# Modulation pieces moved to other stages, a five-bank rotation for the output projection and gate, and a held transpose in a two-block transformer kernel

## The chip, the cores and the metric

The kernel runs on one core of a Trainium2 chip as a single launch. The metric is device time in microseconds (us), the median of several executions. A separate profiled execution gives the trace. TensorE is written PE (its weight loads PEld), VectorE DVE, ScalarE ACT, GpSimd POOL and SyncE SP; SP issues every DMA of this kernel.

## The reference, cut to what matters

The input x is 1024 tokens by 1024 features, all float32. Two blocks follow each other.

```python
def reference(...):
    x = first_block(...)    # one layer
    return second_block(...)  # two layers
# first_block
proj = rms_norm(x, g) @ w_in
ya = diff_attention(...)            # 4 heads, dense
yb = neighbourhood_attention(...)   # 8 heads
x = x + concat(ya, yb) @ w_out
x = x + sigmoid(x @ w_ple_gate) * (p @ w_ple_proj)
# second_block, for l in 0, 1
mod = silu(c) @ w_mod[l] + b_mod[l]          # 1024 -> 6 * 1024
sh1, sc1, gt1, sh2, sc2, gt2 = split(mod, 6)
h = rms_norm(x, g1) * (1 + sc1) + sh1
o = concat(dilated_attention(h), latent_attention(h))
x = x + gt1 * (o @ w_out[l])
h = rms_norm(x, g2) * (1 + sc2) + sh2
x = x + gt2 * (relu(h @ w_mlp_in[l]) ** 2 @ w_mlp_out[l])
```

`mod` has one row, so it is not worth a matrix product on PE: the kernel computes it on DVE.

## The kernel before, in words

Every float32 product runs as three PE products of a high and a low part (`mm3`); ACT makes the high part and DVE or POOL the low part (`split`, `load_w`). One accumulation over 1024 features is 24 matmuls of 512 columns into one PSUM bank. The eight banks are pools of their own: two G (`psum_g`), two S (`psum_s`), one A (`psum_a`), two T and one J (`psum_t`).

The stages in order: attention of the first block; its output projection (`block1_end` calls `out_proj`) and its gate (`halves` with its own `mul`); then for each layer l the dilated heads (`dilated`), the latent heads (`mla`, four pairs hp of two heads), the output projection (`out_proj`), the up projection (`mlp`: two plain products per half, then groups fg 1 to 15) and the down projection (`down_proj`: 35 steps of four 9-matmul runs, then a plain tail).

**Modulation pieces.** `mod_start` fills a list, `background`. For each layer it holds 96 pieces and four sums. A piece (`mod_piece`, L967) loads 256 KB of w_mod into a tile `modraw` and multiplies it by silu(c) with one DVE instruction that also accumulates. A sum (`mod_sum`, L973 and L975) ends a range of pieces with two small matmuls and one or two DVE instructions. The main program takes entries off the list with `run_background(n)`: 36 in the first block, 51 in the latent heads of layer 0 (2 for each of the eight half-heads of hp 0 and 1, 4 for those of hp 2, then 4, 4, 5, 6), 42 in its up groups (3 after each of fg 2 to 15), 10 in its down projection (steps 0 to 9), 51 in the latent heads of layer 1, and the last 10 in its up groups, one after each. The tile a piece uses is `self.mraw`: a ring of two in the latent heads, and the ring of two `raw` tiles from the up groups on.

**The planner.** `TileContext(..., schedule_with_timeline_sim=True)` orders each engine's instructions at build time. The place in the program is an instruction's priority (`high_priority(n)`, used by `ahead`, raises it), and an instruction may be put ahead of others where its tiles and operands are free. On the chip each engine, and SP's queue of DMAs, runs its list in order.

**Output projection and gate.** `out_proj` has 16 groups (8 feature tiles by 2 halves of the tokens). Each loads a tile xo, accumulates 24 matmuls in a G bank and ends with one DVE instruction (L875 in the first block, L877 later) that adds xo. In the first block the same DVE also builds the position tables of the dilated heads: 32 instructions at L1156, each followed by a 256 KB DMA out of a ring of two tiles `tab`. The 16 groups of the gate read the sums of the output projection.

**End of the dilated heads.** The last pair's `dil_merge` weighs the outputs on DVE (L1432), adds them on POOL (L1433, tile `mix`) and returns `put`, eight transposes into two G banks, which `pipeline` runs at its end. `mla_start`, which prepares the first latent pair, comes just ahead of that in the program.

Of the kernel before, what the change touches and what calls it, by code (L numbers as in the profile page):

```python
# [11 lines left out]
F32 = mybir.dt.float32  # L12
# [6 lines left out]
P = 128  # L19
# [114 lines left out]
class Emit:  # L134
# [58 lines left out]
    def psum_s(self, shape=None):  # L193
        return self.psS.tile(shape or [P, 512], F32, tag="S", name="sps")

    def psum_a(self):
        return self.psA.tile([P, 512], F32, tag="A", name="pa")

# [72 lines left out]
    def setup(self):  # L271
        nc = self.nc
        es = self.es
        self.dram = self.pool("dram", es, space=DRAM)
        self.const = self.pool("const", es)
        self.psS = self.pool("psS", es, {"S": 2}, PSUM)
        self.psA = self.pool("psA", es, {"A": 1}, PSUM)
        self.psT = self.pool("psT", es, {"T": 2}, PSUM)
        self.psJ = self.pool("psJ", es, {"J": 1}, PSUM)
        self.scaler = nc.gpsimd  # L280
        self.turn, self.apart = 0, False
        self.psG = self.pool("psG", es, {"G": 2}, PSUM)
        self.hp = self.pool("hp", es)
        self.wp = self.pool("wp", es, {"wh": WB, "wl": WB, "raw": 2})
        self.wring = [self.wp]
        self.st = self.pool("st", es, {"l1": 3, "l2": 3, "r24": 2, "rsy": 2, "rst": 2, "sr": 2, "stw": 2, "stc": 2, **{t: 4 for t in ("mn", "cc", "ssq", "r8")}})
        c = self.const
        self.ident = c.tile([P, P], F32, name="ident")
        make_identity(nc, self.ident)
        self.inv24 = c.tile([P, 24], F32, name="inv24")  # L290
        nc.vector.memset(self.inv24[:, 0:16], 1.0 / 64)
        nc.vector.memset(self.inv24[:, 16:24], 1.0 / 32)
        self.zeros = c.tile([P, 1], F32, name="zeros")
        nc.vector.memset(self.zeros, 0.0)
        self.mixd = [self.dram.tile([8, P, S], F32, name=f"mixd{b}") for b in range(3)]
        self.xTd = [self.A["x_o"]] + [self.dram.tile([8, P, S], F32, name=f"xTd{b}") for b in (1, 2)]
        self.xTm = self.dram.tile([8, P, S], F32, name="xTm")
        self.modd = {}
# [408 lines left out]
        with self.tc.high_priority(n):  # L707
            return f()

    def pipeline(self, groups, lag=1, ahead=(0, 0, 0, 0)):  # L710


        values, finish, put = [], [], None
        for before, scores, val, fin, after in groups:
            for f in before:
                f()
            if put:
                self.ahead(put, ahead[0])
            put = self.ahead(finish.pop(0), ahead[1]) if len(finish) > len(values) else None
            self.ahead(scores, ahead[2])  # L720
            values.append(val)
            finish.append(fin)
            if len(values) > lag:
                self.ahead(values.pop(0), ahead[3])
            for f in after:
                f()
        while values:
            self.ahead(values.pop(0), ahead[3])
            if put:
                self.ahead(put, ahead[0])  # L730
            put = self.ahead(finish.pop(0), ahead[1])
        for f in finish:
            if put:
                self.ahead(put, ahead[0])
            put = self.ahead(f, ahead[1])
        if put:
            self.ahead(put, ahead[0])

# [126 lines left out]
    def out_proj(self, w, b, gate, order, after, step=lambda: None, done=lambda d, half: None, pair=True):  # L865
        nc = self.nc

        def mul(d, half, wt, c0):
            sl = slice(half * 512, half * 512 + 512)
            xo = self.xt.tile([P, 512], F32, tag="xo", name="xo")  # L870
            self.dma(xo, self.xTd[b][d, :, sl])
            ps = self.psum_g()
            self.gemm_t(ps, self.mix, half, wt, 8, c0, order)
            if gate is None:
                nc.vector.tensor_tensor(self.X(d, half), ps, xo, op=OP.add)  # L875
            else:
                nc.vector.scalar_tensor_tensor(self.X(d, half), ps, gate[:, d:d + 1], xo, op0=OP.mult, op1=OP.add)  # L877
                self.dma(self.xTm[d, :, sl], self.X(d, half))
            done(d, half)

        self.halves(w, mul, after, step, self.first_w, pair)
# [9 lines left out]
    def block1_end(self, after):  # L891
        nc = self.nc
        x1 = self.act()

        def split_x(d, half):
            hi, lo = self.act_tile(x1, d, half)
            self.split(hi, lo, self.X(d, half))

        es = ExitStack()
        self.wring = [self.wp] * WB + [self.pool("gw", es, {"wh": 2, "wl": 2})] * 2  # L900
        pp = self.pool("ple", es, {"gth": 3, "pl": 3})
        tables = self.position_tables(es)
        per = -(-len(tables) // 16)

        def side():
            for _ in range(min(per, len(tables))):
                tables.pop(0)()
            if side_steps.pop(0):
                self.run_background(1)

        side_steps = [True] * 4 + [False] * 99
        self.out_proj(self.A["w_out"][0], 0, None, None, lambda half: None, side, split_x, False)

        def mul(d, half, wt, c0):
            sl = slice(half * 512, half * 512 + 512)
            pl = pp.tile([P, 512], F32, tag="pl", name="ple")
            self.dma(pl, self.pled[d, :, sl])
            ps = self.psum_g()
            self.gemm_t(ps, x1, half, wt, 8, c0)
            th = pp.tile([P, 512], F32, tag="gth", name="gth")  # L920
            nc.scalar.activation(th, ps, AF.Tanh, scale=0.5)
            nc.vector.scalar_tensor_tensor(th, th, 1.0, pl, op0=OP.add, op1=OP.mult)
            nc.vector.tensor_tensor(self.X(d, half), self.X(d, half), th, op=OP.add)
            self.dma(self.xTd[1][d, :, sl], self.X(d, half))

        self.halves(self.A["w_ple_gate"][0], mul, after, side)
        self.wring = [self.wp]
        es.close()
# [3 lines left out]
    def mod_start(self):  # L932
# [12 lines left out]
        for l in range(2):  # L945
            m = c.tile([P, 48], F32, name=f"mod{l}")
            self.dma(m, A["bmod"][l])
            self.mod.append(m)
        for l in range(2):
            done = None  # L950
            for t0, t1 in ((0, 16), (16, 24), (24, 40), (40, 48)):
                for t in range(t0, t1):
                    for h in range(2):
                        self.background.append(lambda l=l, t=t, h=h: self.mod_piece(l, t, h))
                        if done and (t, h) == (t0, 1):
                            self.background.append(done)
                done = lambda l=l, t0=t0, t1=t1: self.mod_sum(l, t0, t1)
            self.background.append(done)
# [302 lines left out]

        return [lambda h=h: rope(h) for h in range(2)] + [lambda k=k, h=h: down(k, h) for k in (2, 0, 1) for h in range(2)]

    def dil_v(self, a, l, g):
        s = {}

        def load():
            s["w"] = self.load_w(self.A["w_in_2"][l], [(1024 + g * 256, 256)], 8)

        def step(tt):  # L1270
            ps = self.psum_g([P, 2, 256])
# [126 lines left out]
    def dil_merge(self, l, pr, stw, stc, o):  # L1398
# [25 lines left out]
        nc.vector.tensor_tensor(F, F, a1.unsqueeze(3).to_broadcast([P, 2, 8, 2]), op=OP.mult)  # L1424
        mixes = []
        for half in range(2):
            mix = self.up.tile([P, 4, P], F32, tag="w2k", name="mix")
            hs = slice(4 * half, 4 * half + 4)
            for m in range(2):
                for x in range(2):  # L1430
# [11 lines left out]
    def dilated(self, a, l):  # L1442
# [44 lines left out]
                    yield before if n == 0 else [], *g, after[n]  # L1487

        self.apart = True
        self.pipeline(groups(), 1, (0, 100, 0, 100))  # L1490
        self.apart = False
        es.close()

# [86 lines left out]
    def mla(self, l):  # L1580
# [6 lines left out]
        def groups():  # L1587
            s = self.mla0[0]
            for hp in range(4):
                cur = s  # L1590
# [7 lines left out]
                for m in range(2):  # L1598
                    T, pre = self.mla_heads(2 * hp + m, cur, m)
                    for half in range(2):  # L1600
                        n = 2 if hp < 2 else 4 if hp < 3 or not m else 5 + half
                        yield [pre] if half == 0 else [], *self.mla_group(l, hp, m, half, T, cur), after[2 * m + half] + [lambda n=n: self.run_background(n)]

        self.pipeline(groups(), 1, (0, 60, 0, 60))
        es.close()
# [111 lines left out]
    def mlp(self, l, close, after):  # L1717
# [112 lines left out]
        with ExitStack() as eu:  # L1830
            up = self.pool("uu", eu, {"r": 8})
            up_rest(1, w, *begun[1], up)
            for fg in range(2, 16):
# [4 lines left out]
                else:  # L1838
                    w = wide(A["w_mlp_in_2"][l], 0, 4, fg * 256, 256)
                up_rest(fg, w, *(begun[fg] if fg in begun else up_first(fg, w, up)), up)  # L1840
                self.run_background(1 if l else 3)
        es.close()
        self.es_sr.close()
        self.down_proj(l, us, u0, add_to, after)
# [2 lines left out]
    def down_proj(self, l, us, u0, add_to, after):  # L1847
# [74 lines left out]
        for n, (c, i) in enumerate(seq):  # L1922
# [2 lines left out]
            if n < 3:  # L1925
                load_x(((0, 1, 4, 5), (2, 3, 6, 7))[n > 0], int(n < 2))
            if l == 0:
                self.run_background(int(n < 10))
            for q in range(2):
                for j in range(2):  # L1930
                    if i == 0:
# [39 lines left out]
    def emit(self, stop=None):  # L1971
        with self.es:
# [9 lines left out]
            for l in range(2):  # L1982
# [6 lines left out]
                ex = ExitStack()  # L1989
                self.open_xt(ex)  # L1990
                self.wring = [self.wp] * WB + [Slots(self.hx, [f"b{j}" for j in range(16, 24)])] * 8
                self.out_proj(self.A["w_out_2"][l], 1 + l, self.mod[l][:, 16:24], (0, 1, 2, 6, 3, 4, 5, 7), lambda half: (self.norm_mlp(half, l), half or self.mlp_first(l)))
                self.mlp(l, ex.close, lambda half: l == 0 and self.norm(half, 1, 0, acts[1]))
            es.close()

# [22 lines left out]
```

## Time and profile before

| | us |
|---|---|
| median of 3 runs (lowest, highest) | 3768.87 (3767.29, 3771.7) |
| profiled execution, its own time | 3776.56 |
| profiled execution, span of the trace | 3774.8 |
| PE busy in the span | 3538.3 |
| DVE busy | 2776.9 |
| ACT busy | 1835.6 |
| POOL busy | 1446.2 |

The profiled execution is 7.7 us longer than the median; its span leaves out 1.76 us of its own time. Times inside the span are given in us from its start. In a window of the trace, an engine's idle time is the window's length less its busy time. The granted clock of PE is a share of 2.4 GHz; at the lower of the two levels, 1.2 GHz, it is 0.5.

### The profile page before, as it was taken

The page shows a single profiled execution, that of the slowest core. Times are in us where ns is not written, and L with a number is a line of the kernel's source. Part 1 is how long each engine was busy: PE and PEld are TensorE (multiplying, and loading weights), DVE is VectorE, ACT ScalarE, POOL GpSimd, SP SyncE. Part 2 cuts the span into 40 slices and gives each one's busy share as a digit, 9 for nine tenths or more (in the row PEclk, how much of TensorE's full clock was granted, in tenths as well). Part 3 has the DMA queues.
Part 4 walks back from the last instruction along what each step waited for, and adds up shares of the span by engine and source line. Part 5 has one row for each costly group of instructions (what it writes and reads, how often), then busy time and mean ns, then how long its engine had stood idle before and what let it go on. Part 6 is the DMA issues. An engine that isn't in the chain of part 4 may idle for free. (4 is left out here: it accounts for less than half of the span.)

```text
span 3774.8 us, 59060 instructions
## 1 busy us (share of the span) xinstructions
PE 3538.3 (94%) x20256; PEld 3044.6 (81%) x20256; DVE 2776.9 (74%) x6238; ACT 1835.6 (49%) x3691; POOL 1446.2 (38%) x1155
## 2 busy tenths in 40 slices
PE   7999899989999899998999999899889998999999
PEld 7899899767998778776787887898767876887887
DVE  7888776564666798739867987666798738667986
ACT  5565555533454667624233443455567734333442
POOL 2111232323322223238666553322232236766552
PEclk8999999999999999999999999899999998999999
DMA  7221222463456540134648542455541143448541
GB/s 234 82 54 51 69 72 74 144 196 120 137 171 172 161 123 26 61 116 141 224 154 284 156 147 80 125 160 164 168 129 45 37 131 107 158 152 282 158 146 64
DMA packets 380988, 497.82 MB, mean 132 GB/s; under 512 B 37392, under 2 KB 216592, under 8 KB 380688
## 3 DMA queue, kind: packets, MB, share of 16 engines
q1 hardware_dynamic: 380688, 494.05, 41.9%
q8 instruction: 160, 2.62, 0.3%
q14 instruction: 140, 1.15, 0.1%
HBM read 336.11 MB, written 115.87 MB: 120 GB/s over the span
## 5 line engine op out<-in xcount | busy, mean ns | idle before, releaser
L247 POOL TENSOR_TENSOR wl<-raw,wh 128x512 fp32r<-128x512 f32 (+2 forms) x226 | 291.8, 1302 | 636.7 <-ACT wh L246 540.4
L174 DVE TENSOR_TENSOR pl<-pt,ph 128x512 fp32r<-128x512 f32 (+3 forms) x409 | 269.9, 665 | 66.5 <-ACT ph L173 54.8
L173 ACT CAST ph<-pt 128x512 fp32r<-128x512 f32 (+3 forms) x409 | 227.4, 571 | 143.6 <-PE pt L691 69.0
L246 ACT CAST wh<-raw 128x512 fp32r<-128x512 f32 (+2 forms) x226 | 133.1, 608 | 226.8 <-DMA raw<-in_w_out_dram 56.2
L967 DVE SCALAR_TENSOR_TENSOR modraw<-modraw,csil 128x512 f32<-128x512 f32 x192 | 174.0, 911 | 32.1 <-DMA modraw<-in_wmod_dram 31.4
L1869 ACT CAST wh<-rq 128x768 fp32r<-128x768 f32 x120 | 99.6, 835 | 151.3 <-PE pg L1940 75.2
L1641 ACT ACTIVATE xm<-xm,mn 128x1024 f32<-128x1024 f32 x128 | 148.2, 1158 | 43.4 <-DVE mn L496 43.1
L404 POOL TENSOR_TENSOR qn<-qn,r 128x512 f32<-128x512 f32 x56 | 61.2, 1097 | 267.5 <-DVE r L168 159.6
L496 DVE CUSTOM_DVE_ANT_0 xd<-sps,dtab 128x256 f32<-128x256 f32 (+1 forms) x256 | 101.4, 411 | 79.1 <-PE sps L1329 60.6
L1870 DVE TENSOR_TENSOR wl<-rq,wh 128x768 fp32r<-128x768 f32 x120 | 156.5, 1308 | 0.4 <-ACT wh L1869 0.4
L1696 DVE TENSOR_TENSOR wl<-ssum,wh 128x1024 fp32r<-128x1024 f32 x60 | 120.4, 2007 | 10.7 <-ACT wh L1695 8.1
L698 PE MATMUL pa<-pl,vpm 128*128 128x512 f32 x256 | 111.4, 435 | 8.5 <-DVE pl L174 7.9
L1695 ACT CAST wh<-ssum 128x1024 fp32r<-128x1024 f32 x60 | 62.8, 1047 | 116.3 <-PE pg L1707 43.4
L1695 ACT CAST wh<-sraw 128x512 fp32r<-128x512 f32 (+1 forms) x58 | 48.1, 830 | 137.8 <-PE pg L1707 67.7
L697 PE MATMUL pa<-ph,vpm 128*128 128x512 f32 x256 | 108.5, 424 | 0.6 <-ACT ph L173 0.4
L691 PE MATMUL pt<-ident,xm 128*128 128x128 f32 x692 | 106.9, 273 | 1.4 <-DVE pl L174 0.5
L1736 DVE SCALAR_TENSOR_TENSOR r<-r 128x512 f32<-128x512 f32 x90 | 104.2, 1158 | 2.3
L462 PE MATMUL sps<-ks,qs 128*128 128x512 f32 (+1 forms) x224 | 90.7, 405 | 14.7 <-DVE mn L496 13.4
L691 PEld LDWEIGHTS pt<-ident,xm 128*128 128x128 f32 x692 | 85.7, 140 | 22.1 <-DVE pl L174 1.1
L496 DVE CUSTOM_DVE_ANT_0 xm<-sps,zeros,mn 128x512 f32<-128x512 f32 x128 | 95.1, 743 | 11.3 <-PE sps L223 10.5
L174 DVE TENSOR_TENSOR pl<-pj,ph 128x512 fp32r<-128x512 f32 (+3 forms) x135 | 88.1, 653 | 19.5 <-ACT ph L173 16.8
L538 ACT ACTIVATE x<-x,mn 128x1024 f32<-128x1024 f32 x64 | 73.8, 1153 | 56.2 <-DVE mn L496 53.0
(1675 smaller groups left out, 13966.1 us busy)
## 6 DMA issues: line engine op xcount, KB each, us to landing
modraw<-in_wmod_dram SPq DMA_DIRECT2D x192, 256.0 KB
sraw<-in_w_mlp_in_dram SPq DMA_DIRECT2D x60, 512.0 KB
us<-r SPq DMA_DIRECT2D x120, 256.0 KB
rq<-in_w_mlp_out_dram SPq DMA_DIRECT2D x80, 384.0 KB
raw<-in_w_in_dram SPq DMA_DIRECT2D x194, 128.0 KB
us<-rc SPq DMA_DIRECT2D x90, 256.0 KB
ks<-khh SPq DMA_DIRECT2D x128, 128.0 KB
dtab<-awd SPq DMA_DIRECT2D x32, 512.0 KB
```

What stands on the lines that cost most here:

```text
L173: nc.scalar.copy(hi, src)
L174: nc.vector.tensor_tensor(lo, src, hi.bitcast(F32), op=OP.subtract)
L246: nc.scalar.copy(wh[:, sl], raw)
L247: nc.gpsimd.tensor_tensor(wl[:, sl], raw, wh[:, sl].bitcast(F32), op=OP.subtract)
L496: self.nc.vector.tensor_tensor_reduce(out=dst, in0=src, in1=bias, scale=1.0, scalar=init, op0=OP.add, op1=OP.min, accum_out=mn)
L691: nc.tensor.transpose(ps[:, (i - base) * P:(i - base + 1) * P], X[i][:, c * P:c * P + P], self.ident)
L698: nc.tensor.matmul(ops[:, sl], v(j), pl[:, sl], start=False, stop=last, skip_group_check=True)
L967: nc.vector.scalar_tensor_tensor(raw, raw, 1.0, self.csil, op0=OP.mult, op1=OP.mult, accum_out=self.macc[:, h, t:t + 1])
L1641: nc.scalar.activation(x, x, AF.Exp, scale=-1.0, bias=mn[:, 1:2], accum_out=T["l"][:, i:i + 1])
L1695: nc.scalar.copy(wh[:, 0:m], x)
L1696: (nc.vector if i < 3 else nc.gpsimd).tensor_tensor(wl[:, 0:m], x, wh[:, 0:m].bitcast(F32), op=OP.subtract)
L1870: eng.tensor_tensor(lo, x, hi.bitcast(F32), op=OP.subtract)
```

## The change

Five things change. `psum_w` hands out five banks in turn (S, G, S, A, G), and `out_proj` and the gate use it in place of `psum_g`. The counts of `run_background` change, and the output projections of the second block take pieces too, in a ring of two tiles `u1`. The last `put` of the dilated heads is not run by their `pipeline` but kept in `self.held` and placed behind the first head's `pre` in `mla`, and its `mix` tiles come from the latent pool's ring `x` of four. Two of a layer's sums come two entries later in the list. `dil_v` gets a parameter that no call uses.

```diff
+    def psum_w(self):
+        self.wide_turn = (self.wide_turn + 1) % 5
+        return (self.psum_g, self.psum_s, self.psum_g, self.psum_s, self.psum_a)[self.wide_turn]()
...
-    def pipeline(self, groups, lag=1, ahead=(0, 0, 0, 0)):
+    def pipeline(self, groups, lag=1, ahead=(0, 0, 0, 0), hold=False):
...
+        if hold:
+            return put
         if put:
             self.ahead(put, ahead[0])
...
# out_proj and the gate in block1_end
-            ps = self.psum_g()
+            ps = self.psum_w()
...
# mod_start
-                        if done and (t, h) == (t0, 1):
+                        if done and (t, h) == (t0 + (t0 > 16), 1):
...
# dil_merge
-            mix = self.up.tile([P, 4, P], F32, tag="w2k", name="mix")
+            mix = self.me.tile([P, 4, P], F32, tag="x", name="mix") if pr == 3 else self.up.tile([P, 4, P], F32, tag="w2k", name="mix")
...
# dilated
-        self.pipeline(groups(), 1, (0, 100, 0, 100))
+        self.held = self.pipeline(groups(), 1, (0, 100, 0, 100), True)
...
# mla
-                        n = 2 if hp < 2 else 4 if hp < 3 or not m else 5 + half
-                        yield [pre] if half == 0 else [], *self.mla_group(l, hp, m, half, T, cur), after[2 * m + half] + [lambda n=n: self.run_background(n)]
+                        n = ((0, 0, 3, 4) if l else (0, 1, 4, 5 + m))[hp]
+                        before = [] if half else [pre] if hp or m else [pre, self.held]
+                        yield before, *self.mla_group(l, hp, m, half, T, cur), after[2 * m + half] + [lambda n=n: self.run_background(n)]
...
# mlp, after each fg from 2
-                self.run_background(1 if l else 3)
+                self.run_background((fg > 5) * (1 if l else 4))
...
# down_proj, layer 0, step n
-                self.run_background(int(n < 10))
+                self.run_background(int(2 < n < 34))
...
# emit, each layer
+                self.mraw = (self.mq, "u1")
+                left = [5, 5]
+                def side():
+                    if left:
+                        self.run_background(left.pop())
-                self.out_proj(..., lambda half: (self.norm_mlp(half, l), half or self.mlp_first(l)))
+                self.out_proj(..., lambda half: (self.norm_mlp(half, l), half or self.mlp_first(l)), side)
```

`side` is called after every two groups of the output projection.

## Rows read from the trace of the kernel before

**Rows 1.** The page, part 1: busy time, share of the span and instructions.

```profile
PE 3538.3 (94%) x20256; PEld 3044.6 (81%) x20256; DVE 2776.9 (74%) x6238; ACT 1835.6 (49%) x3691; POOL 1446.2 (38%) x1155
```

**Rows 2.** Windows: length, busy (instructions) by engine, granted clock, DMA share, GB/s.

```profile
755.57:828.13 72.56, 59.40 (x241) 46.60 (x239) 43.01 (x69) 17.13 (x33) 20.24 (x14) 0.95 0.68 220
...
1287.00:1312.00 25.00, 18.20 (x120) 16.38 (x119) 24.15 (x66) 14.53 (x41) 16.68 (x20) 0.80 0.24 77
2722.00:2745.00 23.00, 14.80 (x99) 12.95 (x99) 22.31 (x64) 12.15 (x34) 16.71 (x19) 0.78 0.26 83
1590.00:1677.00 87.00, 85.16 (x391) 69.81 (x390) 30.65 (x49) 24.61 (x41) 29.95 (x24) 1.00 0.39 125
```

**Rows 3.** Windows of the latent heads, up groups and down projection, same columns.

```profile
1300.00:1412.00 112.00, 103.37 (x584) 81.98 (x583) 110.76 (x304) 76.21 (x158) 41.25 (x46) 0.95 0.42 128
...
1737.00:1875.00 138.00, 121.93 (x493) 97.38 (x494) 120.61 (x156) 42.48 (x59) 101.81 (x60) 0.93 0.69 227
1875.00:2025.00 150.00, 150.00 (x663) 124.25 (x662) 93.73 (x73) 47.44 (x68) 98.21 (x70) 1.00 0.49 172
2075.00:2350.00 275.00, 275.00 (x1217) 227.84 (x1216) 225.80 (x267) 108.53 (x165) 131.79 (x73) 1.00 0.40 125
2740.00:2850.00 110.00, 97.79 (x567) 75.81 (x565) 107.53 (x297) 73.83 (x154) 38.20 (x41) 1.00 0.41 122
...
3165.00:3210.00 45.00, 40.35 (x164) 32.09 (x163) 40.86 (x39) 14.37 (x21) 38.93 (x23) 0.92 0.57 187
```

**Rows 4.** Windows of the tile modraw alone: length, DVE busy (two instructions a piece).

```profile
1300.00:1412.00 112.00, 37.72 (x98) 0.95 0.42 128
1737.00:1875.00 138.00, 58.09 (x100) 0.93 0.69 227
2740.00:2853.00 113.00, 37.69 (x98) 1.00 0.40 119
3165.00:3210.00 45.00, 13.52 (x18) 0.92 0.57 187
```

**Rows 5.** Line L967, the piece on DVE: duration ns min/median/max.

```profile
L967 DVE SCALAR_TENSOR_TENSOR modraw<-modraw,csil x192: 656/690/1782, 35.0 to 3201.9; 128x512 f32<-128x512 f32 x192
```

**Rows 6.** Waits from 725 to 940 us: engine line, for whom, total, times, longest.

```profile
DVE tab L1156 <- DMA acd<-tab: 23.5, 18, 3.0
PEld pg L221 <- DVE xT L875: 15.6, 7, 4.1
PE pg L221 <- DVE xT L875: 15.2, 7, 3.7
```

**Rows 7.** PE timeline: first matmuls of output projection groups (start, us, idle before).

```profile
755.57 0.39 PE L221 MATMUL pg<-a01h,wh 128*128 128x512 f32 x1
...
782.64 0.80 PE L221 MATMUL pg<-a01h,wh 128*128 128x512 f32 x1 [3.71 <-DVE xT L875]
...
828.13 0.50 PE L221 MATMUL pg<-a00h,wh 128*128 128x512 f32 x1 [1.32 <-DVE xT L875]
...
844.60 0.39 PE L221 MATMUL pg<-a00h,wh 128*128 128x512 f32 x1
```

**Rows 8.** PE timeline at the end of the dilated heads, layer 0 and layer 1.

```profile
1297.00 1.12 PE L201 MATMUL pg<-ident,mix 128*128 128x128 f32 x4 [3.82 <-POOL mix L1433]
1299.21 1.12 PE L201 MATMUL pg<-ident,mix 128*128 128x128 f32 x4 [1.09 <-POOL mix L1433]
...
2730.76 1.11 PE L201 MATMUL pg<-ident,mix 128*128 128x128 f32 x4 [4.04 <-POOL mix L1433]
2734.97 1.12 PE L201 MATMUL pg<-ident,mix 128*128 128x128 f32 x4 [3.10 <-POOL mix L1433]
```

**Rows 9.** Timeline: first matmuls of the up and down projection of either layer.

```profile
1677.08 0.61 PE L221 MATMUL sps<-a00h,wh 128*128 128x512 f32 x2
...
2036.25 0.50 PE L1940 MATMUL sps<-b24h,wh 128*128 128x512 f32 x1 [1.28 <-ACT wh L1869]
...
3112.68 0.61 PE L221 MATMUL sps<-a00h,wh 128*128 128x512 f32 x2
...
3452.47 0.50 PE L1940 MATMUL sps<-b24h,wh 128*128 128x512 f32 x1 [1.55 <-ACT wh L1869]
```

**Rows 10.** SP's own waits, 1700 to 1900 us.

```profile
SPq L154 <- DVE modraw L967: 66.3, 49, 3.0
```

More of the change, by code (lines that the diff above doesn't have):

```diff
@@ L280, in setup @@
         self.scaler = nc.gpsimd
-        self.turn, self.apart = 0, False
+        self.turn, self.apart, self.wide_turn = 0, False, 0
         self.psG = self.pool("psG", es, {"G": 2}, PSUM)
@@ L917, in mul @@
             self.dma(pl, self.pled[d, :, sl])
-            ps = self.psum_g()
+            ps = self.psum_w()
             self.gemm_t(ps, x1, half, wt, 8, c0)
@@ L1262, in latent_steps, with dil_v @@
         return [lambda h=h: rope(h) for h in range(2)] + [lambda k=k, h=h: down(k, h) for k in (2, 0, 1) for h in range(2)]
-    def dil_v(self, a, l, g):
+    def dil_v(self, a, l, g, pool=None):
         s = {}
         def load():
-            s["w"] = self.load_w(self.A["w_in_2"][l], [(1024 + g * 256, 256)], 8)
+            s["w"] = self.load_w(self.A["w_in_2"][l], [(1024 + g * 256, 256)], 8, pool)
         def step(tt):
@@ L1991, in emit @@
                 self.wring = [self.wp] * WB + [Slots(self.hx, [f"b{j}" for j in range(16, 24)])] * 8
-                self.out_proj(self.A["w_out_2"][l], 1 + l, self.mod[l][:, 16:24], (0, 1, 2, 6, 3, 4, 5, 7), lambda half: (self.norm_mlp(half, l), half or self.mlp_first(l)))
+                self.mraw = (self.mq, "u1")
[3 more added lines that the diff above has]
+                        self.run_background(left.pop())
+                self.out_proj(self.A["w_out_2"][l], 1 + l, self.mod[l][:, 16:24], (0, 1, 2, 6, 3, 4, 5, 7), lambda half: (self.norm_mlp(half, l), half or self.mlp_first(l)), side)
                 self.mlp(l, ex.close, lambda half: l == 0 and self.norm(half, 1, 0, acts[1]))
```

## The prediction, as put on record before the change was run

> **What bounds the kernel now.** I read the page's busy shares first: PE is busy 3538.3 us of 3774.8 [rows 1], so only the other 236 us, and time at PE's lower clock, can be won. Cutting the span into 25 us windows shows where they lie: the output projection of the first block, the end of the dilated heads, the first hundred us of the latent heads, and the norm and first half of the up groups of each layer. The windows named below are those stretches; the waits of PE say who ends the idle time in each, and the windows of the tile modraw show which of them hold pieces. In the out projection of layer 0 PE is busy 85.16 of 87 us and DVE only 30.65 [rows 2]; in the later up groups and the down projection PE is never idle [rows 3]. Little can be won there. A change of 0.2% (7.5 us) is about what a measurement can tell from none.
>
> **Where pieces really run.** This decides most of what follows. The program spreads 42 entries over all up groups of layer 0 and 10 over the first ten steps of its down projection, whose first matmul is at 2036.25 [rows 9]. Yet all 50 pieces (52 entries less two sums) run between 1737 and 1875 [rows 4]. The 49 of a latent stage, two thirds of them written for hp 2 and 3, all run in its first 112 us. So the planner takes a piece as soon as one of its ring's two tiles is free, 160 us and more ahead of its place. I expect the same after the change: counts decide how many pieces a stage gets, not when in it they run. By the list, pieces then number 41 instead of 49 in the latent heads of layer 0, 27 instead of 49 in those of layer 1, 9 and 10 instead of none in the out projections, 68 instead of 50 in up and down of layer 0, and 2 instead of 9 in the up groups of layer 1.
>
> **Five banks, first block: -13 us.** PE waits 15.2 us, seven times, for DVE's L875 to free a G bank, and DVE waits 23.5 us for the DMAs that empty the table tiles [rows 6]. DVE runs in order, so its sums stand behind tables. From 755.57 to 828.13 PE begins eleven groups, ten intervals, 72.56 us; the three from there to 844.60 take 16.47, 5.49 each [rows 7]. Unhindered, ten would take 54.9: 17.7 us are lost, the idle time and the lower clock behind it (0.95 granted [rows 2]). With five banks PE may run four groups ahead, some 22 us, more than that whole lag. What is late next is the gate: its splits overwrite the tiles that the out projection reads, and they need all sums of a half. The tables keep DVE until about 827 as before, then come the last sums and eight splits, so the gate's first matmul moves from 844.60 to about 831, not further. Bounds: -17.7 and 0 (if DVE's order keeps the gate where it is). I take -13, near the lower. The gate and the second block's out projections show no such wait: 0. There one S bank is used again by the first up product, behind a sum that waits for the norm; at most 1.3 us, in the sum as nothing.
>
> **Fewer pieces in the latent heads: -7 us.** While pieces run, DVE is busy 110.76 of 112 us and PE idle 8.6 (layer 0), 107.53 of 110 and 12.2 (layer 1) [rows 3]; behind them PE is nearly full. Forty-nine pieces cost DVE 37.7 us, 0.77 each [rows 4]. If the crowded stretch shortens with the number, layer 0 wins 8/49 of 8.6, 1.4 us, and layer 1 22/49 of 12.2, 5.5 us. Bounds: 0, if PE's gaps come from the score chain; 8 x 0.77 and all 12.2, together -18.4, if DVE alone sets the pace. I take the proportional value, since PE's rate drops evenly over the stretch.
>
> **The held transposes: -3 us.** PE stands 3.82 + 1.09 and 4.04 + 3.10 us for POOL's mix, 12 in all [rows 8], and behind that its clock falls for a time from 2.4 to 1.2 GHz: 0.80 and 0.78 granted on the mean, with 6.8 and 8.2 us idle in those windows [rows 2]. Were all of it won, that would be 15 us idle and some 10 of clock, -25. But DVE is busy 24.15 of 25 and 22.31 of 23 there [rows 2], with the merge and then the norms that the first latent scores need; the change takes nothing off it. PE can only do later matmuls earlier, and they are then missing as filler. Against it: two of the four x tiles stay with mix until its transposes, now behind the first head's, two runs of 1.1 us, +2.2 if the third score waits. I take -3, near the upper bound.
>
> **Up groups: -3 and +3 us.** From first up to first down matmul layer 0 takes 359.2 us, layer 1 339.8 [rows 9]; the same work but 50 pieces against 9 [rows 4]: 19.4/41, 0.47 us a piece. Layer 1 loses 7 pieces, 3.3 us: -3; bounds 0 and -8.2, all idle and clock loss of 3165 to 3210 [rows 3]. Layer 0 gets 18 more. They would follow the others, past 1875, where DVE is busy 93.73 of 150 and PE full [rows 3]; 18 pieces at 58.09/50, 1.16 us, are 21 us and fit into 56. So between 0 and 18 x 0.47 = 8.5; I take +3, because the entries' lower priority helps the first groups a little. A piece also holds up SP, 1.35 us each by 66.3 over 49 [rows 10], with the loads of up weights queued behind.
>
> The price of a piece grows where POOL works: its DVE instruction takes from 656 to 1782 ns [rows 5], 0.77 us with its accumulator read in the latent heads where POOL is busy 41.25 of 112, 1.16 in the up groups where it is 101.81 of 138 [rows 3, 4]. The Trainium skill ("SBUF — State Buffer", Who interferes with whom) says that a DVE instruction with two SBUF inputs and a GpSimd instruction that reads SBUF exclude each other for a whole instruction. By that rule, the trace agreeing in direction, pieces go from the cheap stage to the dear one, which speaks against the change: at the longest time the 18 would cost 32 us, not 3 (rival C).
>
> **The rest: +1 us.** The 19 pieces in the out projections take 14.6 us of DVE at 0.77, beside 56 us of DVE idle time per stage [rows 2]; uncovered they cost 14.6, covered nothing; I take +1, for loads of xo held up in SP's queue, which the extra banks mostly hide. Norm in layer 0 now waits for a sum fed by these pieces, but they begin some 80 us ahead of it. The later sums and the unused parameter: 0, bounded by two short matmuls each.
>
> Sum: -13 - 7 - 3 - 3 + 3 + 1 = -22 us. The profiled execution's 3776.56 would become 3754.6; that execution lies 7.7 above the median, so the median 3768.87 becomes 3746.9, 0.6% faster.
>
> **Rivals.**
> A. The planner leaves the pieces where they are written, from fg 6 on and through the down projection. Then layer 0's up groups win the 19.4 us instead of losing 3. The 31 entries of the down projection cost 36 us of DVE, of the 49 left in its 275 [rows 3], so 0 to 5. Time: 3747 - 22.4 + 3, about 3728. For it: lower priority. Against: rows 4.
> B. Five banks give nothing: DVE, not the bank, paces that stage, because tables are spread over the groups by plan and the gate waits for DVE anyway. 3747 + 13 = 3760. For it: DVE's own 23.5 us of waits [rows 6]; against: DVE is busy only 43.01 of 72.56 [rows 2].
> C. Slower: the 18 added pieces of layer 0 are paid in full, 1.78 us of DVE [rows 5] and 1.35 us of SP [rows 10], because late weights make DVE late again. 18 x 3.13 = 56, so 3747 - 3 + 56 = 3800. It decides from 25/18, 1.4 us a piece. For it: the loads behind SP; against: 0.47 measured, and the slack past 1875.
> D. The change does not do what it says: the planner reorders so that the won idle time turns up elsewhere, DVE being the real limit at each of these places. 3769.
>
> **How the numbers follow.** Forecast 0.50, A 0.17, B 0.15, C 0.09, D 0.09. The predicted time is the forecast's, 3747. The range 3722 to 3768 reaches past A and B and to the lower half of D; left out are C, half of D and some 0.05 under A with a full gain elsewhere, 0.18. Faster by over 0.2%: nearly all of the forecast, A, and two thirds of B (its 3760 is just past the bound): 0.76. Same: the rest of B and most of D: 0.14. Slower: C and a little of D: 0.10.
>
> **What the changed profile would show.** Right: no PE wait on L875; the gate's first matmul about 76 us behind the matmul that is at 755.57 now, not 89; pieces in one unbroken run of about 55 us in the latent heads of layer 1; in layer 0's up groups a run that begins where it did and lasts 45 us longer, with PE nearly full behind 1875. Wrong: pieces seen from fg 6 on or in the down projection (A); PE waiting for L1021 or L174 splits at the gate's start (B); PE idle, and SP waiting on L967, all through layer 0's up groups (C); the same idle time before the first latent scores although the mix wait is gone would show the -3 for the held transposes to be 0.

## The result, and the profile after

The kernel after takes 3741.41 us (median of 4, 3738.1 to 3746.76) beside 3768.08 of the kernel before on the same chip: ratio 0.9928, interval 0.9916 to 0.9941, 27 us less. The forecast was 3747. The profiled execution of after lasts 3736.3 us in span; it is shorter than that of before by 38.5 us, 12 more than the medians differ, so a stage is judged below by several profiles and not by this pair alone.

The first block comes first. PE's timeline of the kernel after: the output projection's first two groups to start, its 4th and 14th, then the gate's first, second and fourth group (start, us, what ended the idle time before):

```profile
717.55 0.39 PE L226 MATMUL sps<-a00h,wh 128*128 128x512 f32 x1
720.72 0.48 PE L226 MATMUL sps<-a01h,wh 128*128 128x512 f32 x1
...
748.72 0.39 PE L226 MATMUL pa<-a01h,wh 128*128 128x512 f32 x1
...
804.78 0.39 PE L226 MATMUL pa<-a00h,wh 128*128 128x512 f32 x1
...
822.08 0.50 PE L226 MATMUL pg<-a00h,wh 128*128 128x512 f32 x1 [0.82 <-ACT a00h L173]
825.66 0.80 PE L227 MATMUL pg<-a00l,wh 128*128 128x512 f32 x1 [3.08 <-DVE a00l L174]
...
834.75 0.39 PE L226 MATMUL sps<-a00h,wh 128*128 128x512 f32 x1
...
847.47 0.40 PE L226 MATMUL pg<-a01h,wh 128*128 128x512 f32 x1
```

In the kernel before, the attention's last product on `pvp`, the output projection's first group and the gate's fourth:

```profile
733.82 0.39 PE L223 MATMUL pg<-pvp,wl 128*128 128x512 f32 x1
734.04 0.39 PE L221 MATMUL pg<-a00h,wh 128*128 128x512 f32 x1
...
860.92 0.39 PE L221 MATMUL pg<-a01h,wh 128*128 128x512 f32 x1
```

The gate begins at 822.08 instead of 844.60 [rows 7], but its first group needs 12.7 us where a group took 5.49: it follows the splits one by one. From the second group on the gain is 15 us (844.60 + 5.49 less 834.75), and 13.4 are left when the dilated heads start. The ten intervals from the 4th to the 14th group, 72.56 us before, take 56.06; from there to the gate's fourth group it is 42.69 us instead of 32.79. Two groups begin in S banks while the attention still runs (its last product on `pvp` is at 740.77); in the kernel before, the first began behind it. The waits of 720 to 950 us (engine, line, for whom, total, times, longest), PE's longest and DVE's for the tables:

```profile
PE pg L227 <- DVE a00l L174: 3.1, 1, 3.1
PE pg L226 <- ACT a50h L1023: 2.7, 1, 2.7
```

```profile
DVE tab L1163 <- DMA acd<-tab: 16.6, 14, 2.7
```

The 15.2 us for a bank [rows 6] are gone, and what is late next is DVE's split, as foreseen. This wait on L174 is also a sign that the prediction named for rival B; B's time did not come. At the end of the dilated heads of layer 0 and 1, PE's timeline:

```profile
1281.87 1.12 PE L206 MATMUL pg<-ident,mix 128*128 128x128 f32 x4 [3.83 <-POOL mix L1440]
1284.07 1.12 PE L206 MATMUL pg<-ident,mix 128*128 128x128 f32 x4 [1.08 <-POOL mix L1440]
...
2708.73 1.03 PE L206 MATMUL pg<-ident,mix 128*128 128x128 f32 x4 [4.02 <-POOL mix L1440]
2712.94 1.12 PE L206 MATMUL pg<-ident,mix 128*128 128x128 f32 x4 [3.18 <-POOL mix L1440]
```

These are the four waits of [rows 8], to 0.1 us: the planner put the held transposes back where they had been. The windows of the tile modraw show where the pieces run (window, length, DVE busy, two instructions a piece):

```profile
1288.00:1376.00 88.00, 30.38 (x82) 0.99 0.41 125
...
1712.00:1890.00 178.00, 74.37 (x127) 0.92 0.68 222
...
2706.00:2769.00 63.00, 19.19 (x48) 0.95 0.42 129
...
3100.00:3150.00 50.00, 1.93 (x4) 0.86 0.27 89
```

All 41 pieces of the latent heads of layer 0 run in their first 90 us, 24 of 27 in layer 1 within 63 us (the other three follow later, so it is not quite the one run foretold), 2 in its up groups, and 63 of the 68 late ones of layer 0 before 1890 (the last five by 1898), though 31 entries are written in the down projection from 2027 on. So the planner pulls them ahead as before [rows 4]. Behind 1875 (1854 here, where the up groups start 21 us earlier) PE is not full as forecast: windows of the up groups of layer 0 (length, busy by engine PE, PEld, DVE, ACT, POOL, granted clock):

```profile
1750.00:1800.00 50.00, 43.48 (x177) 34.07 (x176) 44.01 (x57) 15.23 (x22) 37.36 (x23) 0.93 0.66 210
1800.00:1850.00 50.00, 43.76 (x175) 34.37 (x174) 40.35 (x61) 13.04 (x18) 30.60 (x18) 0.93 0.68 224
1850.00:1900.00 50.00, 44.66 (x180) 35.56 (x179) 43.15 (x61) 14.54 (x22) 30.39 (x19) 0.93 0.70 228
1900.00:1950.00 50.00, 50.00 (x223) 41.41 (x222) 32.03 (x25) 15.86 (x23) 39.70 (x27) 1.00 0.49 175
```

As long as pieces run, PE idles some 6 us in 50 at 0.93 of the clock; where they end, it is full.

### The profile page after: what moved, and what is told of

Same layout as the page of the kernel before. It is cut to its first block, busy times and chain, and to the rows that moved or that the text cites. A ratio compares the mean times of both kernels' runs of the same rounds, so it can differ in the third digit from the quotient of the medians.

```text
span 3736.3 us, 59053 instructions
## 1 busy us (share of the span) xinstructions
PE 3514.1 (94%) x20256; PEld 3029.1 (81%) x20256; DVE 2783.9 (75%) x6238; ACT 1831.4 (49%) x3691; POOL 1448.1 (39%) x1155
## 4 chain that ended last, share of the span: by engine, by line
PE 64%; DVE 17%; DMA 8%; issue 5%; ACT 3%; POOL 2%; SPq 1%; DVEq 0%; POOLq 0%; ACTq 0%
PE sps L1715 7%; PE pg L226 6%; PE pg L228 6%; PE pg L227 6%; PE pg L1715 5%; PE sps L1948 4%; PE pg L1948 3%; PE pt L1948 3%; PE sps L227 2%; PE sps L226 2%; PE sps L228 2%; DVE modraw L974 2%; DMA modraw<-in_wmod_dram 2%; PE pt L206 2%; PE pt L696 2%
## 5 line engine op out<-in xcount | busy, mean ns | idle before, releaser
L174 DVE TENSOR_TENSOR pl<-pt,ph 128x512 fp32r<-128x512 f32 (+3 forms) x407 | 268.9, 665 | 82.0 <-ACT ph L173 70.4
L174 DVE TENSOR_TENSOR pl<-pj,ph 128x512 fp32r<-128x512 f32 (+3 forms) x137 | 89.6, 654 | 30.8 <-ACT ph L173 25.7
L1734 ACT COPY keep<-sps 128x512 f32<-128x512 f32 x60 | 35.1, 586 | 140.5 <-PE sps L1715 131.0
```

What stands on the lines that cost most here:

```text
L174: nc.vector.tensor_tensor(lo, src, hi.bitcast(F32), op=OP.subtract)
```

## The stages of every kernel

The landmarks are matmuls whose start PE's timeline gives in each profile. "dil0" is the start of layer 0's dilated heads; each further column is the time from the landmark before: to the first latent transposes (lat), the first wide product of the up groups (up), the first down matmul, the dilated heads of layer 1, and the same again to the end. A column is thus headed by the landmark that ends it: "down0" is the length of layer 0's up groups, "dil1" of its down projection, "lat1" of layer 1's dilated heads, "up1" of its latent heads with the output projection. In us:

```
kernel            dil0  lat0   up0 down0  dil1  lat1   up1 down1   end
before           932.6 368.8 394.5 340.3 326.6 374.3 393.2 322.1 322.3
before_again     925.5 370.3 394.5 342.0 325.6 372.3 394.0 321.0 321.4
banks_only       913.7 367.0 391.9 344.5 326.1 368.4 390.8 321.3 321.2
hold_only        929.3 366.2 393.7 340.7 326.8 362.0 394.7 320.7 321.8
counts_only      927.8 368.0 391.0 351.8 326.1 364.2 381.8 319.3 322.4
no_hold          916.5 367.4 390.3 349.9 327.4 366.1 382.6 318.8 321.2
after            919.2 367.1 388.6 351.8 325.6 361.7 382.8 317.9 321.8
pieces_in_place  916.1 372.9 390.9 322.3 332.4 360.0 382.4 319.4 322.3
in_place_latent  917.0 374.1 388.4 320.7 332.7 364.7 386.7 318.7 321.2
in_place_gate    922.7 373.7 387.6 319.0 332.5 366.6 382.2 320.1 322.3
no_late_pieces   918.6 370.6 388.9 319.6 327.3 363.2 382.9 321.2 324.1
late_pieces_dma  921.1 370.5 390.5 335.3 326.2 363.8 384.5 318.9 321.2
late_pieces_dve  920.8 367.5 391.1 356.1 326.4 359.0 386.5 319.8 322.5
no_latent_pieces 919.1 371.7 377.1 351.1 327.6 369.9 377.7 318.8 321.3
```

## The experiments

**The kernel before again, and each part of the change alone.** The first is the kernel before unchanged. `banks_only` is before with `psum_w` in the two projections, `hold_only` with the kept `put` and its tiles, `counts_only` with the counts, the later sums and the pieces in the output projections.

```diff
# banks_only
-            ps = self.psum_g()
+            ps = self.psum_w()
...
# hold_only
-        self.pipeline(groups(), 1, (0, 100, 0, 100))
+        self.held = self.pipeline(groups(), 1, (0, 100, 0, 100), True)
...
# counts_only
-                self.run_background(1 if l else 3)
+                self.run_background((fg > 5) * (1 if l else 4))
...
```

> The kernel before once more, unchanged. The profiles of before and after differ by 38.5 us in span, the medians only by 26.7. Theory chance: some 8 to 12 us of the profile's difference, above all the 11 us in the dilated heads of layer 1, where the change edits nothing, belong to the one execution that was profiled; then this profile shows dilated layer 1 (norm's transposes to the first latent transposes) shorter by 8 us or more than the 377.6 us of the profile before, and a span near 3766. Rival, planner: the changed program orders dilated layer 1 differently and wins there; then this profile repeats 377.6 within 3 us, and the span is near 3775 or other stages vary by as much.

> Five banks alone, all else as before. Theory (the bank wait is the stage's limit, the gate follows): 13 us less than before, about 3755, 0.9965; gate's first matmul some 22 us earlier, the a50h wait of layer 0's dilated heads 13 us earlier. Rival B (DVE's order paces the stage): within 3 us of before.

> The held transposes alone. Theory now, from the profile after: the planner puts the transposes of the last mix back where they were, so PE waits for POOL's mix 3.8 + 1.1 and 4.0 + 3.1 us as before, and the time is within 2 us of before. Forecast on record: 3 us less. Rival: the transposes move behind the first head's in one layer and 8 us or more are won.

> The new counts of pieces alone (latent heads 41 and 27, output projections 9 and 10, up and down of layer 0 68, up of layer 1 2), with two G banks and no held transposes. By the forecast's terms: -7 +0 +1 = 6 us less than before, 3762. By the stages of the profile after: latent heads with output projection -4.9 and -10.5, up groups +10.4 and -4.1, together 9 us less, 3759. Rival C (late pieces are paid in full): slower than before by 10 us or more. Rival, no effect (what one stage wins another loses): within 3 us.

Measured: before again 3768.71 us, ratio 0.9999 (0.9989 to 1.0008); banks 3750.51, 0.9950 (0.9937 to 0.9962); held transposes 3763.49, 0.9989 (0.9979 to 0.9998); counts 3755.6, 0.9966 (0.9954 to 0.9979). The repeated profile is 8.2 us shorter, 7 of it in the first block, which varies by that much between kernels with the same code there. It is not the dilated heads of layer 1: 374.3 and 372.3 are alike, and the theory of chance falls for that stage. Rival B falls too: the banks give 18. Each part wins more than was expected of it (13, at most 2, and 6 to 9 us).

The parts alone sum to 37 us by the medians, together they give 27. The table says why: with held transposes alone layer 1's dilated heads take 362.0, with counts alone 364.2, with both 361.7, against 368.4 to 374.3 with neither. The same 8 us or so are counted with each of these two parts, and some 5 with the banks. Two windows of 50 us at the same distance from the start of that stage, first of the kernel before again, then of the held transposes alone:

```profile
2607.90:2657.90 50.00, 46.42 (x254) 38.24 (x253) 28.72 (x106) 21.65 (x60) 9.21 (x18) 0.93 0.47 133
```

```profile
2606.80:2656.80 50.00, 47.03 (x281) 39.59 (x280) 35.78 (x132) 26.02 (x73) 10.06 (x18) 1.00 0.60 166
```

In nearly the same busy time PE completes 281 matmuls against 254 (381 against 391 in the 50 us before), DVE 132 instructions against 106: another order of the stage's work, and a clock that does not fall. PE's timelines show the order. The sequence of its matmuls in this stage is nearly the same in `before`, `before_again` and `no_latent_pieces` (374.3, 372.3 and 369.9 us), and nearly the same in `after`, `pieces_in_place`, `in_place_latent`, `no_late_pieces` and `late_pieces_dma` (360.0 to 364.7), but it differs between these two sets. The counts edit no code of that stage, the kept `put` only its last pair. Which step of the planner's choice makes the better order stays open.

**Is the price of a late piece that of being pulled ahead?** `pieces_in_place` is after, with each late piece of layer 0 tied on DVE's queue behind the last square or sum of its place (`mark`). The other three leave out the 68 late pieces, their products, or their loads.

```diff
# pieces_in_place, mod_piece (mark: the last square, in down_proj the last sum)
+        with self.tc.issue_after(self.mark) if self.late else ExitStack():
             nc.vector.scalar_tensor_tensor(raw, raw, 1.0, self.csil, op0=OP.mult, op1=OP.mult, accum_out=self.macc[:, h, t:t + 1])
...
# no_late_pieces
+        if self.late:
+            return
...
# late_pieces_dma, in place of the product
+        if self.late:
+            nc.vector.tensor_copy(self.macc[:, h, t:t + 1], raw[:, 0:1])
+            return
...
# late_pieces_dve, without the load
-        self.dma(raw, self.A["wmod"][l, t, h])
+        src = self.csil if self.late else raw
+        if not self.late:
+            self.dma(raw, self.A["wmod"][l, t, h])
...
+        nc.vector.scalar_tensor_tensor(raw, src, 1.0, self.csil, op0=OP.mult, op1=OP.mult, accum_out=self.macc[:, h, t:t + 1])
```

> The kernel after, but in up and down of layer 0 each piece's DVE instruction must follow the last DVE square or sum of its place in the program, so that no piece is pulled ahead. This makes rival A's condition true. Rival A: the up groups shorten from 351.8 us (first wide product to first down matmul) to about 325, the down projection stays at 326 plus at most 5, and the time is 20 us or more below the kernel after, near 3720. Rival to it, DVE of the down projection: with DVE 85 to 90% busy there, 31 pieces of 0.8 us or more are paid in full, 10 to 25 us, and the time is within 8 us of the kernel after. Third: a waiting piece holds DVE's queue and SP's weight loads, and the time is above the kernel after.

> The kernel after with the 68 pieces of up and down of layer 0 left out (their modulations keep the bias alone). If each piece costs what the two layers' up groups say, (351.8 - 318)/66 = 0.5 us, the up groups fall from 351.8 to about 318 us, and the rest of the profile stays. If the forecast was right that only the first 50 pieces cost (0.47) and those behind 1875 are hidden, the up groups fall by 24 to 27 us, to 325 or more.

> The kernel after with the 256 KB loads of the 68 late pieces kept, but their DVE product reduced to a copy of one column. Theory DVE (the piece's product of 0.7 to 1.8 us holds DVE while the first up groups wait for it): up groups near 318 to 322 us, as with no pieces. Rival SP and DMA (the loads hold up the loads of weights): up groups stay at 345 to 352.

> The kernel after with the DVE products of the 68 late pieces kept, but taken from a tile that is already in SBUF: their 68 loads are left out. Theory DVE: up groups stay at 345 to 352 us. Rival SP and DMA: up groups near 318 to 325. If both this run and the one with loads alone fall about half way, the price is in the two together (DVE waiting for late loads).

Measured: in place 3720.7 us, ratio 0.9869 (0.9853 to 0.9886), 21 us below after: rival A's 3728 with its condition made true. The others ran once: 3718.06, 3733.64 and 3751.37. The up groups of layer 0 take 351.8 us with all pieces pulled ahead, 319.6 without them, 322.3 with all of them in place. So pulled ahead 68 pieces cost 32 us, and the expectation of about 318 us without them holds. In place they cost 3 us here and some 5 in the down projection, which takes 332.4 us against 327.3 without late pieces and 325.6 in after, where all of them ran before it. (It takes 332.4 to 332.7 in the three kernels with pieces in place, 325.6 to 327.6 in the other eleven.) Together 351.8 + 325.6 us became 322.3 + 332.4, 23 less. Waits of PE in the up groups of layer 0, after (first fence) and in place (second), the longest of those for DVE:

```profile
PE sps L1715 <- DVE wl L1704: 9.6, 5, 3.0
PE pg L226 <- DVE r L1743: 6.0, 1, 6.0
PE pt L980 <- DVE modraw L974: 3.0, 2, 1.8
PE pg L1715 <- DVE r L1743: 2.9, 2, 2.1
PE sps L1715 <- DVE r L1743: 2.5, 3, 1.3
```

```profile
PE pg L226 <- DVE r L1744: 6.0, 1, 6.0
PE sps L1716 <- DVE b18l L1087: 3.4, 1, 3.4
```

The waits for `wl`, the weights' split, and for the later squares are gone: pieces pulled ahead stood before them. Below is the longest wait for `wl` in after, 3.01 us, first DVE's timeline and then PE's: a piece, which itself waits for its load, stands ahead of the split.

```profile
1830.60 1.37 DVE L974 SCALAR_TENSOR_TENSOR modraw<-modraw,csil 128x512 f32<-128x512 f32 x1 [1.69 <-DMA modraw<-in_wmod_dram]
...
1831.90 2.27 DVE L1704 TENSOR_TENSOR wl<-sraw,wh 128x1024 fp32r<-128x1024 f32 x1
```

```profile
1834.23 0.50 PE L1715 MATMUL sps<-a00h,wl 128*128 128x512 f32 x1 [3.01 <-DVE wl L1704]
```

From 1750 to 1900 PE of after idles 18.1 us in all, and 0.07 of the clock over 150 us is some 10 us more, by estimate. Together this is nearly the 29.5 us between after and in place. The tie also changes the order of PE's matmuls there; what that alone does no run shows. And the windows of the kernel in place, with PE full, then its pieces alone in up and down:

```profile
1800.00:1850.00 50.00, 50.00 (x222) 41.44 (x221) 36.81 (x35) 15.21 (x22) 33.23 (x24) 1.00 0.44 149
1850.00:1900.00 50.00, 50.00 (x225) 41.44 (x224) 43.16 (x44) 17.83 (x25) 38.70 (x24) 1.00 0.66 224
1900.00:1950.00 50.00, 50.00 (x222) 41.44 (x221) 42.21 (x44) 16.92 (x24) 39.36 (x25) 1.00 0.58 190
```

```profile
1810.00:2000.00 190.00, 47.02 (x70) 1.00 0.64 217
2000.00:2300.00 300.00, 34.03 (x66) 0.98 0.56 180
```

DVE is as busy from 1850 to 1900 as in the kernel after (43.16 and 43.15), but PE is full instead of 44.66 of 50. A piece even takes longer, 47.02/35 = 1.34 us. Neither DVE's total nor a piece's length sets the price; what stands behind it in DVE's queue does. The split between load and product: loads alone 15.7 us over no pieces, products alone 36.5, both 32.2. So the two do not add up. Loads alone fit neither theory's range (318 to 322, 345 to 352); without loads to wait for, the products run closer together than in after, all between 1723 and 1833. In the kernel with loads alone the 68 copies take 10.3 us of DVE, 0.15 each, yet DVE stood still for the loads (waits of 1682 to 2017):

```profile
DVE macc L976 <- DMA modraw<-in_wmod_dram: 71.9, 54, 3.4
```

The Trainium skill ("PSUM — Partial Sum Buffer", Engine vs sequencer instructions) says that VectorE's queue is strictly first in, first out. The trace agrees: the copies of 0.15 us wait up to 3.4 us for their loads, and what stands behind them waits too. Below, the sum `r` that is squared next starts only behind such a copy; PE has waited 2.36 us for it.

```profile
1818.82 0.15 DVE L976 COPY macc<-modraw 128x1 f32<-128x1 f32 x1 [1.42 <-DMA modraw<-in_wmod_dram]
1818.93 0.69 DVE L1747 TENSOR_TENSOR r<-sps,keep 128x512 f32<-128x512 f32 x1
```

```profile
1819.67 0.57 PE L1719 MATMUL sps<-a41h,wh 128*128 128x512 f32 x1 [2.36 <-DVE r L1747]
```

**Are the held transposes needed, and can the place be chosen elsewhere?** `no_hold` is after without them. `in_place_latent` ties the latent heads' pieces to the reciprocal of their group as well, `in_place_gate` moves 24 late entries of the list (23 pieces and a sum) to the first block's gate; both build on `pieces_in_place`.

```diff
# in_place_latent: late is set during mla
+            self.mark = nc.vector.reciprocal(T["r"][:, hs], T["l"][:, hs]).ins
...
# in_place_gate, at each of the gate's eight steps, pieces in the ring pl
+            self.run_background(3)
```

> Five banks and new counts without the held transposes. Forecast on record: the held transposes are worth 3 us, so 3744. Theory now: they move nothing at the place where they are written (PE waits for mix as before); what the profile of the held transposes alone won, 10 us in the dilated heads of layer 1, is another order that the planner finds there, and the new counts alone already bring it (364 us against 368 to 374 without either). So this kernel has dilated layer 1 at 364 us or less and a time within 4 us of the kernel after. Rival: the held transposes are needed, dilated layer 1 is back at 370 or more and the time is 3750.

> The pieces held at their places in up and down of layer 0, as before, and also in the latent heads, where each piece's DVE instruction must follow the reciprocal of its group of scores. If the crowding of the first 60 to 90 us of the latent heads is what makes PE idle there (7 us in layer 0 and 6 in layer 1 of the profile after), the time falls by 5 to 12 us from the 3720.7 with up and down alone. If those gaps come from the chain of scores, it stays within 4 us. If DVE, busy 20 to 22 of 25 us in the later groups, is late there instead, it rises.

> The pieces held at their places in up and down of layer 0, and 24 of them moved to the gate of the first block, where DVE is busy 6 to 13 of 25 us; up and down keep 44. If the 32 pieces in the down projection cost the 6 us by which that stage is longer (332.4 against 326) and the gate hides its 24, 3 to 6 us less than 3720.7. If the gate's PE is then made to wait for DVE or for the pl tiles that the pieces share, its stage is longer by 5 us or more and the time is 3722 or above.

Measured: without held transposes 3742.27 us, 0.9938 (0.9924 to 0.9953), not to be told from after; the dilated heads of layer 1 at 366.1, 2 us more than expected, but below the 368 to 374. With the latent pieces in place 3716.69, 0.9868 (0.9849 to 0.9887), the same as 0.9869. PE is fuller in the first hundred us, and pays in the second (96.45 against 98.34) and third; windows of the latent heads of layer 0 from their start, first with those pieces pulled ahead (`pieces_in_place`), then in place:

```profile
1289.00:1389.00 100.00, 88.45 (x507) 69.22 (x507) 97.75 (x270) 65.26 (x136) 39.15 (x40) 0.99 0.39 113
...
1489.00:1589.00 100.00, 97.47 (x553) 80.59 (x552) 69.07 (x152) 65.18 (x119) 21.83 (x21) 1.00 0.15 48
```

```profile
1291.00:1391.00 100.00, 96.63 (x576) 81.44 (x576) 84.76 (x212) 74.77 (x160) 31.91 (x45) 0.95 0.05 16
...
1491.00:1591.00 100.00, 92.64 (x512) 74.43 (x511) 80.16 (x189) 60.02 (x108) 22.35 (x20) 1.00 0.35 108
```

With pieces at the gate: 3730.78, 0.9908 (0.9894 to 0.9923), 10 us above the same kernel without them: dil0 is 6.6 us later, and the dilated heads of layer 1, again in another stage than the edit's, 6.6 longer. The planner put 19 of the 23 pieces behind 850 us, among the norm's sums, and PE waits 8.3 us for DVE's last square sum, in one wait:

```profile
PE pt L206 <- DVE nsq L1002: 8.3, 1, 8.3
```

**What the pieces of the latent heads cost.** The kernel after with its 41 and 27 latent pieces left out.

```diff
# no_latent_pieces, mod_piece (late: set during mla)
+        if self.late:
+            return
```

> The kernel after with the 41 and 27 pieces of the latent heads left out (their modulations keep the bias alone). From the first latent transposes to the first wide product of the up groups the kernel after takes 388.6 us in layer 0 and 382.8 in layer 1. If the forecast's price holds there (5.5 us for 22 pieces in layer 1, 0.25 each; 0.18 each in layer 0), these fall to 381 and 376. If the price is what layer 1 of the kernels with old and new counts says, (393 - 382)/22 = 0.5 each, they fall to 368 and 369. If DVE alone sets the pace there, at 0.77 each, to 357 and 362. Stages of two kernels with the same code differ by up to 3 us.

Measured once: 3736.15 us; 377.1 and 377.7 us instead of 388.6 and 382.8. That is 11.5/41 = 0.28 and 5.1/27 = 0.19 us a piece. In layer 1 it is near the forecast's 0.25; in layer 0 it lies between its 0.18 and 0.5. The 22 pieces above these 27 cost 11 us, 0.5 each (393.2 to 394.7 against 381.8 to 382.8). The price seems to rise with the number, perhaps since the first ones fall into gaps; that is not shown. The eight kernels with these pieces pulled ahead, after among them, take 387.6 to 391.1 us in layer 0 and 381.8 to 386.5 in layer 1. So both falls lie outside what such a stage varies, the second by 4 us and in one execution.

## Why the prediction was right, point by point

The time fell by 27 us where 22 were forecast, but its terms were off on both sides and made up for one another. By the means of the table, where several kernels have the same code:

- Where the pieces run, and their numbers: right to the piece, and the run in layer 0 lasts 48 us longer (1712 to 1898, 186 us against 138) where 45 were foretold. Rival A's order was not the planner's.
- Five banks, first block: -13 forecast; dil0 falls from 928.8 (four profiles) to 918.0 (nine with the banks and no pieces at the gate), -11, in its bounds. The bank waits were right: by the means of these profiles the ten intervals win 16.7 us, where 17.7 were taken as lost. The step "the gate's first matmul moves from 844.60 to about 831, not further" was not: it moves further, to 822.08, and then follows the splits, which gives back 11 us up to its fourth group where the forecast had 4.7. Luck made up for it: two groups start ahead, during the attention, so the 4th group comes 60.0 instead of 65.6 us behind the attention's first matmul on `pvp`, 5.7 us that no term held. That the second block gains nothing by the banks is not refuted: with the banks alone its latent heads and output projection shrink by about 2 and 3 us, but with the new counts the banks change them by -1 and +1 (`counts_only` to `no_hold`).
- Fewer pieces in the latent heads: -7 forecast; counts alone give -3 in layer 0 and -12 in layer 1 (with the 9 and 10 pieces that the output projections now hold), inside the bound of -18.4. "If the crowded stretch shortens with the number" was the step mis-sized: the last 22 pieces of layer 1 cost some 0.5 each, twice what it took.
- Held transposes: -3 forecast, 0 found at their place. PE's waits for mix are all there. The sign named ahead ("the same idle time before the first latent scores") is what the profile shows, though the sign supposed the mix wait gone, and it never went. The 5 us that they win alone (interval up to 0.9998) lie in the dilated heads of layer 1; with banks and counts they win nothing that can be told.
- Up groups: layer 1 -3 forecast, -2 found. Layer 0 +3 forecast, +9 found (341.9 to 351.2), just past the bound of 8.5. The failed step is "18 pieces at 58.09/50, 1.16 us, are 21 us and fit into 56": DVE had the time, but pulled ahead a piece costs by what waits behind it, and the 18 added ones cost 0.5 each, no less than the 50 before them (22.3/50 = 0.45 over no pieces, close to the 0.47 forecast).
- Not in the forecast: -8 in the dilated heads of layer 1, by another order. That the total came within 6 us of the forecast owes something to luck.
- Rest +1: not seen by itself.

With the latent heads and output projections of after and of `no_hold` at -5 and -11, the found terms sum to -11 - 5 + 9 - 8 - 11 - 2 = -28, the measured 27. Rival C is refuted: 18 pieces cost 9 us, not 56. Rival D holds for the held transposes alone.

## What to carry to other kernels

A planner that takes work as soon as its buffer is free makes a filler's place in the program void: the count written for a stage sets how many pieces it gets, the free tiles of the ring set when. Tie the filler to an instruction of its place on its own engine, and do it where PE does not wait for that engine next: here that was worth 21 us, nearly as much as the whole change. An engine's free time in a stage does not tell what added work costs; ask what stands behind it in the queue.

## What was not expected

A piece whose product is nearly nothing still cost 0.2 us of the stage (15.7/68), because DVE waits in its queue for a 256 KB load. And edits elsewhere moved a stage that they hardly touch by 8 us; what the trace shows of it is another order of PE's matmuls, 281 against 254 in 50 us, and a granted clock of 1.00 against 0.93 there.
